# Gate projections of a decoder layer: each pass as two matmuls on the two row halves of TensorE's array

## The chip, the cores and the metric

The kernel runs on one core of one Trainium2 chip. The metric is the device time of one execution in microseconds (us). The profile's engines are PE (TensorE's matmuls), PEld (TensorE's loads of stationary weights), DVE (VectorE), ACT (ScalarE), POOL (GpSimd) and SP (the engine that issues most DMAs).

## The reference

One layer of a decoder trunk, with 512 tokens of 1024 channels, all in float32:

```python
h = rms_norm(x, g_pre_mix)
q, k, v, cb, cc, cu, ga, gc = split(h @ w_in)      # 512 x 6, then 1024 x 2 columns
y_attn = stick_breaking_attention(q, k, v) @ w_attn_out
y_conv = (cb * causal_depthwise_conv(cc * cu, w_conv)) @ w_conv_out
gate_attn, gate_conv = split(sigmoid(concat([ga, gc]) + b_gate))
x = x + rms_norm((gate_attn * y_attn + gate_conv * y_conv) @ w_o, g_post_mix)
x = x + rms_norm(square(relu(rms_norm(x, g_pre_mlp) @ w_up)) @ w_down, g_post_mlp)
x = x + sigmoid(rms_norm(x, g_ple) @ w_ple_gate) * (p @ w_ple_proj)
```

The change is in `ga` and `gc`: `h` (512 x 1024) times columns 3072 to 5119 of `w_in`.

## The kernel before, in words

Float32 precision is reached with three passes of a reduced format (float32r). Each operand is split into a high part, rounded to float32r by ScalarE, and a low part, the rest, made by VectorE (`split`, L63 to L65). A product is then high x high, high x low and low x high, added up in PSUM: `mm3`, whose three matmuls are lines L89, L90 and L91 wherever they are issued from.

`h` is held transposed, with channels on the 128 partitions and the 512 tokens along the free dimension, as eight blocks of 128 channels; `hx(k)` gives the high and low part of block k (`h1h` and `h1l` in the profile). `wcols` loads 128 columns of a weight matrix, eight blocks of 128x128, with one DMA into `raw` and splits them into `whi` and `wlo`. `proj` takes a bank of PSUM and runs the 8 x 3 = 24 matmuls of one projection onto it: the stationary operand is a 128x128 block of weights, the moving one 128x512 of `h`, and the contraction is over all 128 rows of the array.

`gate(j, which)` (L398 to L402) is one such projection for output channels 128j to 128j+127 of `ga` (which = 0) or `gc` (which = 1), and a sigmoid with its bias that ScalarE reads straight from the bank into an SBUF tile `tmp` (L401). There are 16 gates. The two of j = 0 are placed in the last round of the attention loop (L421 and L426). The others are in the mixing loop, `for j in range(NK)` at L448, which runs in this order: the gates of j, an output projection of the convolution branch (12 matmuls, `py`, L458) whose bank is multiplied into the gate by L459, an output projection of the attention branch (12 matmuls, L462) with L463, the addition of both (L464) and the split into `mh` and `ml` (L465). For j = 1 the first gate comes earlier, between the two output projections of j = 0 (L461), and the second at its own place; for j = 2 to 7 both gates stand side by side.

The order of TensorE's and SP's instructions is as written (`manual_schedule`); that of the other engines is drawn up by the framework's scheduler from its own costs. PSUM has eight banks, all given out in turn by `bank()`; `tm()` gives out one of five SBUF tiles of 128x512. In the mixing loop GpSimd also forms differences of `w_down` blocks (`make_sums`, L296), which are written to DRAM for a later stage. After the loop come eight transposes of the per-layer input (L477, their banks emptied by the split into `pt`) and the rows of W_o (`rows`, L481), whose first round takes all eight banks.

Of the kernel before, what the change touches and what calls it, by code (L numbers as in the profile page):

```python
# [12 lines left out]
ALU = mybir.AluOpType  # L13
# [3 lines left out]
P = 128  # L17
# [3 lines left out]
NK = D // P  # L21
# [12 lines left out]
def hybrid_block(ctx, tc, x, p, g_pre_mix, w_in, b_gate, w_conv, w_attn_out, w_conv_out, w_o,  # L34
                 g_post_mix, g_pre_mlp, w_up, w_down, g_post_mlp, g_ple, w_ple_gate, w_ple_proj, out):
    nc = tc.nc
# [4 lines left out]
    w_in, w_conv, w_attn_out, w_conv_out = w_in[0], w_conv[0], w_attn_out[0], w_conv_out[0]  # L41
# [15 lines left out]
    def bank():  # L57
        return psp.tile([P, 512], F32, tag="ps", name="ps")

    def tm(dt=F32):  # L60
        return tmp.tile([P, 512], dt, tag="tmp", name="tmp")
# [5 lines left out]
    def weights(loads, shape):  # L67
        raw = raws.tile(shape, F32, tag="raw", name="raw")
        for sel, src in loads(raw):
            nc.sync.dma_start(sel, src)  # L70
        lo = wts.tile(shape, F32R, tag="w", name="wlo")
        hi = wts.tile(shape, F32R, tag="w", name="whi")
        half = shape[1] // 2
        for sl in (slice(0, half), slice(half, 2 * half)):
            split(hi[:, sl], lo[:, sl], raw[:, sl])
        return hi, lo
# [4 lines left out]
    def wcols(w, c0):  # L81
        src = w[:, c0:c0 + P].rearrange("(k p) m -> p k m", p=P)
        return weights(lambda t: [(t, src)], [P, NK, P])
# [4 lines left out]
    def mm3(ps, lh, ll, rh, rl, start, stop, onto=False):  # L88
        nc.tensor.matmul(ps, lh, rh, start=start, stop=False, skip_group_check=onto)  # L89
        nc.tensor.matmul(ps, lh, rl, start=False, stop=False, skip_group_check=onto)  # L90
        nc.tensor.matmul(ps, ll, rh, start=False, stop=stop, skip_group_check=onto)  # L91

    def proj(w, xs, nk=NK, k0=0):
        ps = bank()
        for k in range(nk):
            xh, xl = xs(k)
            mm3(ps, w[0][:, k0 + k], w[1][:, k0 + k], xh, xl, k == 0, k == nk - 1)
        return ps
# [41 lines left out]
    def mov(hp):  # L140
        return lambda k: (hp[0][k // 4][:, k % 4, :], hp[1][k // 4][:, k % 4, :])
# [116 lines left out]
    for t in range(2, NT):  # L258
        ps = bank()
# [9 lines left out]
    hx = mov(h1)  # L269
# [126 lines left out]
        split(oy_h[1][:, c], oy_l[1][:, c], y)  # L396

    def gate(j, which):  # L398
        ps = proj(wcols(w_in, 3072 + 1024 * which + j * P), hx)
        sg = tm()  # L400
        nc.scalar.activation(sg, ps, AF.Sigmoid, bias=cols[:, 8 * which + j:8 * which + j + 1])  # L401
        return sg  # L402
# [9 lines left out]
    for j in range(4):  # L412
        wa = scores(st[0])
        wb = scores(st[1])
        y = conv_u(j, ct)
        conv_b(j, y)
        ta = wtrans(wa)
        if j < 3:
            st = proj_q(j + 1)
        else:  # L420
            sg[0] = gate(0, 0)  # L421
        tb = wtrans(wb)
        if j < 3:
            proj_k(j + 1, st)
        else:
            sg[1] = gate(0, 1)  # L426
        of = tm()
        with tc.high_priority(-LATE):
            make_sums(nc.vector)
        av(2 * j, ta, of)  # L430
        av(2 * j + 1, tb, of)
        if j < 3:
            ct = conv_c(j + 1)
# [14 lines left out]
    for j in range(NK):  # L448
        make_sums()
        sa, sc = sg if j == 0 else (next_gate if j == 1 else gate(j, 0), gate(j, 1))  # L450

        def two(t, j=j):
# [20 lines left out]
        if j == 7:  # L473
            for kk in range(2):
                ps = bank()
# [88 lines left out]
    for t in range(NT):  # L564
        tok = slice(t * P, (t + 1) * P)
        for h_ in range(2):
            cs = slice(h_ * 512, (h_ + 1) * 512)
            ps = bank()
# [21 lines left out]
    for half in range(2):  # L590
        ns = slice(half * 256, (half + 1) * 256)
        for c in (0, NJ):
# [3 lines left out]
            for k in range(NK):  # L596
                xh, xl = hm(k)
# [256 lines left out]
    for t in range(2, NT):  # L854
        for cs in CUTS[t]:
            ps = bank()[:, 0:cs.stop - cs.start]
# [31 lines left out]
```

## Time and profile before

| what | value |
|---|---|
| median of 2 runs | 746.5 us (746.45 to 746.55) |
| profiled execution, device time | 746.06 us |
| its span, first to last instruction | 744.0 us |
| mean granted TensorE clock | 0.993 |
| matmuls / weight loads | 3936 / 3936 |
| TensorE matmul busy | 730.5 us |
| VectorE busy | 539.1 us |
| ScalarE busy | 396.2 us |

The device time is 2.1 us longer than the span, since it holds what lies around the first and the last instruction. In the profile's rows, busy time is the sum of shown durations; matmuls are pipelined, so one matmul's shown duration is longer than the distance to the next one's start, and the distance between starts (the pitch) is what counts for time. Rows of the order in time give the start and the duration in us, the engine, the line, the operation, the tiles (written <- read), rows*columns of the array, shape and count; what stands in brackets is the engine's idle time before it and what ended that.

### The profile page before, as it was taken

Reading aid. Unit: us, or ns where it says so; the run is one execution under the profiler, and the core shown is the slowest. Engines: PE = TensorE matmul, PEld = TensorE weight load, DVE = VectorE, ACT = ScalarE, POOL = GpSimd, SP = SyncE. Lnnn points to the kernel's source line nnn. Section 1 sums busy time; section 2 is a strip of 40 time slices with the busy share of each in tenths; the row PEclk is TensorE's granted clock in tenths of the full one; section 3 lists DMA queues with packets and bytes.
Section 4 is the critical chain, followed back from the end, with each engine's and each line's share of the span. In section 5 each row is a group of like instructions: output and inputs, shape, how many; then the busy total and the mean of one; then the engine's idle time right before and its main releaser. Section 6 shows DMA issues by size and latency. Waiting matters only on the chain.

```text
span 744.0 us, 10442 instructions
## 1 busy us (share of the span) xinstructions
PE 730.5 (98%) x3936; PEld 632.4 (85%) x3936; DVE 539.1 (72%) x747; ACT 396.2 (53%) x672; POOL 108.0 (15%) x131
## 2 busy tenths in 40 slices
PE   7999999998999999999999999999999999999997
PEld 6888788887888888878899999999988888888876
DVE  4889898959755424554869879977699878268762
ACT  6555656462533322442855776867776476256531
POOL 0005051347425222200100000000000000001100
PEclk8999999999999999999999999999999999999999
DMA  8393727157599885752244444432555767577311
GB/s 310 126 327 107 221 100 227 54 199 252 178 346 273 254 281 193 269 161 57 106 178 112 115 115 114 118 110 86 168 160 174 224 243 230 174 245 263 128 58 58
DMA packets 112107, 132.30 MB, mean 178 GB/s; under 512 B 4116, under 2 KB 82744, under 8 KB 111032
## 3 DMA queue, kind: packets, MB, share of 16 engines
q1 hardware_dynamic: 111480, 127.44, 53.8%
q10 hardware_dynamic: 576, 4.19, 1.4%
q8 instruction: 31, 0.51, 0.3%
q14 instruction: 20, 0.16, 0.1%
HBM read 108.55 MB, written 23.07 MB: 177 GB/s over the span
## 4 chain that ended last, share of the span: by engine, by line
PE 82%; DVE 6%; DMA 5%; ACT 3%; POOL 2%; issue 1%; SPq 1%; DVEq 0%; POOLq 0%; ACTq 0%
PE ps L89 26%; PE ps L90 26%; PE ps L91 26%; DVE wlo L65 1%; DMA w<-in_w_down_dram 1%; DMA raw<-wsum 1%; PE ps L368 1%; POOL w L296 1%; DMA xin<-in_x_dram 1%; DMA wsum<-w 1%; DMA raw<-in_w_o_dram 1%; ACT whi L64 1%; DVE keep L338 1%; PE ps L354 1%; PE ps L548 1%
## 5 line engine op out<-in xcount | busy, mean ns | idle before, releaser
L65 DVE TENSOR_TENSOR wlo<-raw,whi 128x512 fp32r<-128x512 f32 x120 | 89.4, 776 | 45.8 <-ACT whi L64 19.7
L89 PE MATMUL ps<-h1h,whi 128*128 128x512 f32 x288 | 113.8, 395 | 2.7 <-DVE tmp L395 2.7
L91 PE MATMUL ps<-h1h,wlo 128*128 128x512 f32 x288 | 112.8, 392 | 0.0
L90 PE MATMUL ps<-h1l,whi 128*128 128x512 f32 x288 | 112.7, 391 | 0.0
L64 ACT CAST whi<-raw 128x512 fp32r<-128x512 f32 x120 | 69.1, 638 | 49.6 <-DMA raw<-in_w_in_dram 16.0
L89 PE MATMUL ps<-w,sb 128*128 128x512 f32 x216 | 84.1, 389 | 0.0
L91 PE MATMUL ps<-w,sb 128*128 128x512 f32 x216 | 84.0, 389 | 0.0
L90 PE MATMUL ps<-w,sb 128*128 128x512 f32 x216 | 84.0, 389 | 0.0
L65 DVE TENSOR_TENSOR w<-raw,w 128x1024 fp32r<-128x1024 f32 x56 | 67.7, 1222 | 22.0 <-PE ps L90 11.6
L64 ACT CAST w<-raw 128x1024 fp32r<-128x1024 f32 x56 | 58.4, 1051 | 37.5 <-DMA raw<-wsum 13.4
L125 POOL TENSOR_TENSOR rs<-ms,mhalf 128x1 f32<-128x1 f32 x20 | 14.5, 726 | 409.0 <-DVE ms L121 367.6
L89 PEld LDWEIGHTS ps<-h1h,whi 128*128 128x128 f32 x288 | 54.5, 189 | 13.8 <-DVE tmp L395 2.9
L91 PEld LDWEIGHTS ps<-h1h,wlo 128*128 128x128 f32 x288 | 54.3, 189 | 11.5
L90 PEld LDWEIGHTS ps<-h1l,whi 128*128 128x128 f32 x288 | 54.6, 189 | 11.0
L89 PE MATMUL ps<-h2h,us 128*128 128x256 f32 x224 | 63.5, 283 | 0.0
L90 PE MATMUL ps<-h2l,us 128*128 128x256 f32 x224 | 63.4, 283 | 0.0
L91 PE MATMUL ps<-h2h,us 128*128 128x256 f32 x224 | 63.4, 283 | 0.0
L65 DVE TENSOR_TENSOR us<-raw,us 128x1024 fp32r<-128x1024 f32 x42 | 50.7, 1219 | 7.9 <-ACT us L64 7.7
L64 ACT CAST us<-raw 128x1024 fp32r<-128x1024 f32 x42 | 43.4, 1050 | 19.1 <-DVE raw L647 7.5
L89 PE MATMUL ps<-tb,us 128*128 128x256 f32 x168 | 47.9, 285 | 0.0
L90 PEld LDWEIGHTS ps<-w,sb 128*128 128x128 f32 x216 | 40.5, 188 | 8.5
L89 PEld LDWEIGHTS ps<-w,sb 128*128 128x128 f32 x216 | 40.5, 188 | 8.4
(206 smaller groups left out, 1715.6 us busy)
## 6 DMA issues: line engine op xcount, KB each, us to landing
raw<-in_w_in_dram SPq DMA_DIRECT2D x36, 512.0 KB, 6.9
w<-in_w_down_dram SPq DMA_DIRECT2D x32, 512.0 KB, 4.3
wsum<-w SPq DMA_DIRECT2D x32, 512.0 KB, 3.8
raw<-in_w_up_dram SPq DMA_DIRECT2D x32, 512.0 KB, 4.5
raw<-wsum SPq DMA_DIRECT2D x32, 512.0 KB, 5.1
raw<-in_w_down_dram SPq DMA_DIRECT2D x24, 512.0 KB, 4.3
raw<-in_w_o_dram SPq DMA_DIRECT2D x8, 512.0 KB, 6.0
raw<-in_w_ple_gate_dram SPq DMA_DIRECT2D x8, 512.0 KB, 6.7
```

The lines of the kernel that those rows point to most:

```text
L64: nc.scalar.copy(hi, src)
L65: nc.vector.tensor_tensor(lo, src, hi.bitcast(F32), op=ALU.subtract)
L89: nc.tensor.matmul(ps, lh, rh, start=start, stop=False, skip_group_check=onto)
L90: nc.tensor.matmul(ps, lh, rl, start=False, stop=False, skip_group_check=onto)
L91: nc.tensor.matmul(ps, ll, rh, start=False, stop=stop, skip_group_check=onto)
L125: nc.gpsimd.tensor_tensor(r, m, mhalf, op=ALU.pow)
L296: eng.tensor_tensor(r, x_, y_, op=ALU.subtract)
L338: nc.vector.tensor_tensor_scan(kr, kr, kr, 1.0, op0=ALU.mult, op1=ALU.bypass)
L354: nc.tensor.transpose(ps[:, c0 + (qb - kb) * P:c0 + (qb - kb + 1) * P], w[:, o:o + P], ident)
L368: nc.tensor.matmul(ps[:, kb * P:S], lhs, wt[i][:, c0:c0 + n], start=(kb == 0 and i == 0), stop=(kb == NT - 1 and i == 1))
L548: nc.tensor.transpose(ps[:, i * P:(i + 1) * P], hn1[t][g][:, i * P:(i + 1) * P], ident)
```

## The change

For all gates but the two of j = 0, the eight blocks' three passes are issued as two matmuls each: one over contraction rows 0 to 63, one over rows 64 to 127, with the same 128 output channels and 512 tokens. The first half of the rows adds up in one PSUM bank, the second in another. ScalarE then copies the first bank to an SBUF tile, VectorE adds the second bank to it, and the sigmoid reads that tile in place of the bank.

```diff
     def gate(j, which):
-        ps = proj(wcols(w_in, 3072 + 1024 * which + j * P), hx)
+        w = wcols(w_in, 3072 + 1024 * which + j * P)
+        if j == 0:
+            ps = proj(w, hx)
+        else:
+            part = [bank(), bank()]
+            for k in range(NK):
+                xh, xl = hx(k)
+                for i, (lhs, rhs) in enumerate(((w[0][:, k], xh), (w[0][:, k], xl), (w[1][:, k], xh))):
+                    for h in range(2):
+                        rows_ = slice(64 * h, 64 * h + 64)
+                        nc.tensor.matmul(part[h], lhs[rows_], rhs[rows_], start=(k == 0 and i == 0),
+                                         stop=(k == NK - 1 and i == 2))
+            ps = tm()
+            nc.scalar.copy(ps, part[0])
+            nc.vector.tensor_tensor(ps, part[1], ps, op=ALU.add)
         sg = tm()
         nc.scalar.activation(sg, ps, AF.Sigmoid, bias=cols[:, 8 * which + j:8 * which + j + 1])
         return sg
```

The loads, the DMAs and the split of the weights stay as they are; the order of the gates and projections does too.

## The prediction

> **What bounds the kernel now.** I read the page's busy table and its chain first, then the busy time of each engine by stage, then the order in time of single matmuls inside one gate.
>
> ```profile
> span 744.0 us, 10442 instructions
> ...
> PE 730.5 (98%) x3936; PEld 632.4 (85%) x3936; DVE 539.1 (72%) x747; ACT 396.2 (53%) x672; POOL 108.0 (15%) x131
> ...
> PE 82%; DVE 6%; DMA 5%; ACT 3%; POOL 2%; issue 1%; SPq 1%; DVEq 0%; POOLq 0%; ACTq 0%
> ```
>
> TensorE is busy for 98% of the span and carries 82% of the chain that ended last. A busy TensorE says little by itself, so the stage and the pitch (start to start) have to be seen. Of the 16 gates, the two with j = 0 run before 200 us and stay as they are; the other 14 lie between 200 and 312 us.
>
> ```profile
> core 0: us, PE busy (x) PEld busy (x) DVE busy (x) ACT busy (x) POOL busy (x), PEclk, DMA share, GB/s
> 186.00:200.00 14.00, 13.87 (x61) 11.18 (x60) 13.94 (x19) 9.82 (x19) 6.38 (x4) 0.93 0.72 231
> 200.00:312.00 112.00, 112.00 (x495) 92.74 (x495) 51.96 (x66) 35.04 (x58) 36.70 (x28) 1.00 0.79 256
> ```
>
> In this stage TensorE never pauses (112.00 of 112.00 us, full clock), while VectorE is busy for 51.96 us and ScalarE for 35.04 us of it. Whatever the change adds to TensorE here goes straight into the end of the kernel; what it adds to the other two has 60 and 77 us of idle time to lie in. Now one gate, that of j = 1, first and last matmul with the weight loads between them:
>
> ```profile
> 205.95 0.39 PE L89 MATMUL ps<-h1h,whi 128*128 128x512 f32 x1
> 205.96 0.19 PEld L90 LDWEIGHTS ps<-h1l,whi 128*128 128x128 f32 x1
> ...
> 206.18 0.39 PE L90 MATMUL ps<-h1l,whi 128*128 128x512 f32 x1
> 206.18 0.19 PEld L91 LDWEIGHTS ps<-h1h,wlo 128*128 128x128 f32 x1
> 206.41 0.39 PE L91 MATMUL ps<-h1h,wlo 128*128 128x512 f32 x1
> ...
> 211.17 0.39 PE L91 MATMUL ps<-h1h,wlo 128*128 128x512 f32 x1
> ...
> 211.39 0.39 PE L89 MATMUL ps<-oyh,whi 128*128 128x512 f32 x1
> ```
>
> The gate is 24 matmuls (8 blocks of contraction rows, three passes each) from 205.95 to 211.39: 5.44 us, a **pitch of 0.2267 us** a pass. The 0.39 us shown for one is its whole way through the array, of which 0.16 us lies under the next. Each load starts as the matmul before it starts, lies wholly beside it, and costs nothing. The 14 changed gates hold 14 x 24 = 336 passes, 76.2 us.
>
> **The change, part by part.** Each pass becomes two loads and two matmuls of 64 rows and the same 512 columns. No instruction with 64 contraction rows is in this trace, so whether the two run beside each other can't be read from it; all of the argument is in bounds. Per pass two costs must be held apart: the streaming of 512 columns, and the loads.
>
> Streaming, from the matmuls of 256 columns in the up projection, 12 of them from the first row to the last:
>
> ```profile
> 420.37 0.28 PE L89 MATMUL ps<-h2h,us 128*128 128x256 f32 x1
> ...
> 421.81 0.28 PE L89 MATMUL ps<-tb,us 128*128 128x256 f32 x1
> ```
>
> 1.44 / 12 = 0.120 us. So 256 columns more cost 0.1067 us, 512 columns 0.213 us, and 0.0133 us is fixed for each matmul. If the halves stream beside each other, a pass can't take less than 0.213 us (336 x 0.0133 = 4.5 us gained) and, if both fixed parts are paid one after the other, takes 0.240 us (4.5 us lost).
>
> Loads, from the place where they are the limit, the short matmuls of attention:
>
> ```profile
> 153.81 0.19 PEld L368 LDWEIGHTS ps<-wth,v 128*128 128x128 f32 x1
> 153.93 0.23 PE L368 MATMUL ps<-wth,v 128*128 128x128 f32 x1
> 153.93 0.19 PEld L368 LDWEIGHTS ps<-wtl,v 128*128 128x128 f32 x1
> 153.99 0.27 PE L368 MATMUL ps<-wtl,v 128*128 128x128 f32 x1
> 154.04 0.19 PEld L368 LDWEIGHTS ps<-wth,v 128*128 128x128 f32 x1
> 154.10 0.44 PE L368 MATMUL ps<-wth,v 128*128 128x512 f32 x1
> 154.16 0.19 PEld L368 LDWEIGHTS ps<-wtl,v 128*128 128x128 f32 x1
> ...
> 154.38 0.39 PE L368 MATMUL ps<-wtl,v 128*128 128x512 f32 x1
> ```
>
> Loads follow each other at 0.11 to 0.12 us, although each is shown as 0.19, and a matmul may start 0.06 us after its load started. Two loads in a pass, with 128 columns each as now, take 0.22 to 0.23 us at this rate if fewer rows make them no shorter: **just inside** the 0.2267 us. A workable order exists: the matmul of the upper half starts, the lower half's load runs for 0.11 us, its matmul starts, the upper half's next load runs for 0.11 us, and then the upper half's stream is just done. So for overlapping halves I take a pass at 0.2267 us, **0 us**, with -4.5 and +4.5 as ends. The row nearest to it, the 256-column one, keeps 0.120 us with a load each; two of these would be 0.240, the upper end, but there the streaming sets the pitch, which here is shared.
>
> Switches between whole-height and half-height work: j = 1 has its two gates apart, between output projections, j = 2 to 7 side by side, so 2 x 8 = 16 entries and exits. Least 0; at most the array empties (0.39 - 0.2267 = 0.16 us) and the next load follows unhidden (0.19 us), 0.35 us. Between these ends I take the emptying alone, with the load under it, as the loads lie in the gate's rows: 16 x 0.16 = **2.6 us** (0 to 5.6). The Trainium skill ("TensorEngine Tiling (Array Packing)", Key Properties) states that a change of the tiling mode drains TensorE; by it 2.6 us is the least of this term, where rows of a stream that never breaks would give 0 and a sum 2.6 us lower. No row here shows such a switch.
>
> Taking the sum out of the banks: each gate adds a ScalarE copy and a VectorE addition of 128x512 and makes the sigmoid wait for both.
>
> ```profile
> L380 ACT COPY tmp<-ps x4: 586/587/590, 55.6 to 162.4; 128x512 f32<-128x512 f32 x4
> ...
> L463 DVE TENSOR_TENSOR tmp<-tmp,ps x8: 680/686/689, 206.2 to 317.6; 128x512 f32<-128x512 f32 x8
> ...
> L401 ACT ACTIVATE tmp<-ps,cols x16: 679/689/695, 188.2 to 309.5; 128x512 f32<-128x512 f32 x16
> ```
>
> 14 x 0.587 = 8.2 us on ScalarE and 14 x 0.686 = 9.6 us on VectorE, in idle time of 77 and 60 us. The sigmoid comes about 1.3 us later than now; its user, the product L459, needs the output projection of 12 passes (2.7 us) behind the second gate anyway. While ScalarE waits with copy and sigmoid, the casts of the next weights (L64) are queued behind them, and their users are matmuls a gate or more later. TensorE waits in this stretch for nothing now, and the banks, six a round in place of four, come round only after eight: the first gate's two are written again by the next round's second gate, 72 passes or 16 us after they are full, and need some 2 us to be read. The one place without cover is the first rows of W_o:
>
> ```profile
> PE ps L89 <- DVE tmp L395: 2.7, 1, 2.7
> ...
> PE ps L89 <- DVE pt L65: 0.2, 1, 0.2
> ```
>
> ```profile
> 312.30 0.69 DVE L459 TENSOR_TENSOR tmp<-tmp,ps 128x512 f32<-128x512 f32 x1 [0.45 <-PE ps L91]
> 315.07 2.58 DVE L65 TENSOR_TENSOR wlo<-raw,whi 128x512 fp32r<-128x512 f32 x4 [2.08 <-ACT whi L64]
> ```
>
> TensorE waits there 0.2 us for a bank that VectorE empties. Both additions of j = 7 (1.4 us) fall ahead of the 2.08 us in which VectorE idles for the weights of W_o, so they cost **0**; if they land behind it, 1.4 us. Less than nothing is possible too, since ScalarE's and VectorE's order is drawn up anew: the 2.7 us wait at about 190 us, and the 7% of clock lost in 186 to 200 us (1.0 us), could go; in the other direction such a wait could arise anew.
>
> Sum: 0 + 2.6 + 0 = 2.6 us on the profiled execution's 746.06 us, 748.7; the median of the runs, 746.5, is 0.4 above that execution, so **749 us**. Its own range: 746.5 - 4.5 = 742 below, 746.5 + 4.5 + 5.6 + 1.4 = 758 above.
>
> **The rivals.**
>
> Serial halves, **slower**. If the second half's matmul starts only when the first has streamed, because the array takes one matmul at a time or the operands' rows don't give each half a place of its own (the change then doesn't do what it says), each pass is two of 0.2267 us: 336 x 0.2267 = 76.2 us, 822.7, with the switches 825. For it: in the rows above no matmul starts before the columns of the one ahead have streamed; the 128-column ones, 0.06 us apart, are merely short. Against it: every matmul there takes all the rows, so that none had a free place to start in; with half the rows free, the order worked out above needs nothing but that TensorE uses them. The Trainium skill ("TensorE: Matmul & The Clock Gate", Part 3, The mechanism) has matmuls on different row groups start about 4 ns apart and overlap; by it a pass costs nothing more, and no run so far shows it.
>
> Exposed loads, **slower**. If in half-height work a load may not lie beside a matmul of its own half, each half's turn is a stream and a load, 0.2267 + 0.11 us, also when the halves overlap: 336 x 0.11 = 37.0 us, with the switches 786 us. Against it stands that at 205.96 the load starts 0.01 us after a matmul on the same rows and costs nothing. The same section of the Trainium skill says that loads overlap with matmuls in flight only when the row group differs, which is this rival's rule; this trace contradicts it for whole-height work and shows nothing for halves.
>
> From 0.271 us a pass (15 us over 336 passes) the result leaves the 2%. Something between is a fourth case: if loads come late, as for the matmul shown at 154.10, whose next starts 0.28 us after it, a pass costs 0.053 us more, 18 us in all, 765 us and up. A gain over 2% would need 15 us; streaming alone gives 4.5 us at most, and the lost waits 3.7 us.
>
> **How the numbers follow.** Overlap at 749 us: 0.60. Serial, 825 us: 0.20. Exposed loads, 786 us: 0.14. Something between: 0.04. Over 2% faster: 0.02. The range reaches from the forecast's low end past the exposed loads with the forecast's upper bounds in part, 742 to 790, and leaves out the serial case and the gain. Two per cent, 15 us, is about what a measurement of this kernel can tell from no change; within it lies only the overlap, 0.60, and slower are the three others, 0.38.
>
> **What would show it.** Overlap: in a changed gate, matmuls of 64 rows start 48 to a gate within 5.4 to 5.8 us, the two of a pass side by side or some 0.11 us apart, and the stage from 200 us on keeps its 112 us but for a few. Serial: matmuls 0.227 us apart all along, a gate of 10.9 us. Exposed loads: gates of about 8.1 us, each load starting after the stream of its own half. Switches: a gap over 0.227 us at the first and last matmul of a gate. The additions are wrong as costed if TensorE waits in the stage for L459, for the copies or for a bank. The forecast falls with one row: halves of one pass that never overlap.

## The result, and the profile after

The changed kernel takes 750.4 us (median of 750.0 and 750.9) against 746.5 us: ratio 1.0061, 95% interval 1.0036 to 1.0085. That is no change by the 2% of the forecast, and 4 us of loss that the interval can tell from nothing. The forecast was 749 us, its range 742 to 790 us.

First the page after: the span, the busy table, the chain.

```profile
span 749.1 us, 11169 instructions
...
PE 734.4 (98%) x4272; PEld 630.6 (84%) x4272; DVE 551.2 (74%) x761; ACT 405.5 (54%) x686; POOL 109.2 (15%) x131
...
PE 80%; DVE 6%; DMA 6%; POOL 2%; ACT 2%; issue 2%; SPq 1%; POOLq 0%; DVEq 0%; ACTq 0%
```

There are 336 matmuls more (4272 for 3936), and TensorE's busy time rises by 3.9 us only. The gate of j = 1 in order of time, in the view that holds TensorE's matmuls and loads; x2 joins two instructions that start together, and 64*128 is rows*columns of the array:

```profile
206.24 0.39 PE L91 MATMUL ps<-oyh,wlo 128*128 128x512 f32 x1
206.55 0.18 PEld L409 LDWEIGHTS ps<-h1h,whi 64*128 64x128 f32 x2 [0.35 <-PE ps L90]
206.56 0.50 PE L409 MATMUL ps<-h1h,whi 64*128 64x512 f32 x2
206.66 0.19 PEld L409 LDWEIGHTS ps<-h1l,whi 64*128 64x128 f32 x2
...
206.89 0.40 PE L409 MATMUL ps<-h1l,whi 64*128 64x512 f32 x2
...
211.70 0.39 PE L409 MATMUL ps<-h1l,whi 64*128 64x512 f32 x2
...
211.92 0.39 PE L409 MATMUL ps<-h1h,wlo 64*128 64x512 f32 x2
212.24 0.19 PEld L89 LDWEIGHTS ps<-oyh,whi 128*128 128x128 f32 x1 [0.35 <-PE ps L409]
212.24 0.50 PE L89 MATMUL ps<-oyh,whi 128*128 128x512 f32 x1
212.35 0.19 PEld L90 LDWEIGHTS ps<-oyl,whi 128*128 128x128 f32 x1
...
212.58 0.40 PE L90 MATMUL ps<-oyl,whi 128*128 128x512 f32 x1
```

The two matmuls of a pass start together, and so do their two loads: **the halves overlap in full**. At the gate's end a pass is 0.22 to 0.23 us, as before. The gate takes 206.56 to 212.24 = 5.68 us in place of 5.44, and the 0.24 us sit at its edges. At an entry or exit the next matmul starts 0.32 us after the last one in place of 0.227, and its load starts only with it (before, it started a matmul earlier), so that this load isn't hidden: the matmul's row is 0.50 us long in place of 0.39, and the matmul behind it comes 0.33 to 0.34 us later, 0.11 us more than in the stream.

To see where the 4 us are, I set every pass of TensorE against the same pass of before (the two halves of a pass as one). The difference of their start times is 0.02 us at the last pass ahead of the first changed gate and 3.96 us behind the last: **16 switches at 0.247 us, 3.95 us**, and nothing between them. It then grows to 5.90 us in the first round of W_o, 1.94 us more, and falls to 5.20 us by the end. W_o's start, in TensorE's waits and in the order of ScalarE and VectorE:

```profile
PE ps L89 <- DVE pt L65: 0.8, 1, 0.8
...
PE ps L89 <- DVE tmp L473: 0.5, 1, 0.5
...
PE ps L89 <- DVE tmp L477: 0.2, 1, 0.2
```

```profile
310.29 1.91 ACT L64 CAST wph<-wpr 128x2048 fp32r<-128x2048 f32 x1
317.15 1.14 ACT L64 CAST whi<-raw 128x512 fp32r<-128x512 f32 x2 [4.95 <-DMA raw<-in_w_o_dram]
318.52 1.14 ACT L64 CAST whi<-raw 128x512 fp32r<-128x512 f32 x2 [0.24 <-DMA raw<-in_w_o_dram]
319.57 0.58 ACT L412 COPY tmp<-ps 128x512 f32<-128x512 f32 x1
```

```profile
317.80 2.67 DVE L65 TENSOR_TENSOR wlo<-raw,whi 128x512 fp32r<-128x512 f32 x4 [2.92 <-ACT whi L64]
320.39 0.68 DVE L413 TENSOR_TENSOR tmp<-ps,tmp 128x512 f32<-128x512 f32 x1
322.26 0.69 DVE L473 TENSOR_TENSOR tmp<-tmp,ps 128x512 f32<-128x512 f32 x1 [1.19 <-ACT tmp L415]
```

The last gate's first whole-height successor starts at 313.1 us, so both its banks are full by then; yet ScalarE copies the first at 319.57 (L412), because the casts of W_o's rows are queued ahead of it and the engine idles 4.95 us for their DMA. The addition (L413), the sigmoid and the two products (L473, L477) that free banks come late in a row, and TensorE waits for the banks of W_o's first round.

### The profile page after: what moved, and what is told of

Its sections match the earlier page's. It is cut to its first block, busy times and chain, and to the rows that moved or that the text cites. A ratio compares the mean times of both kernels' runs of the same rounds, so it can differ in the third digit from the quotient of the medians.

```text
span 749.1 us, 11169 instructions
## 1 busy us (share of the span) xinstructions
PE 734.4 (98%) x4272; PEld 630.6 (84%) x4272; DVE 551.2 (74%) x761; ACT 405.5 (54%) x686; POOL 109.2 (15%) x131
## 4 chain that ended last, share of the span: by engine, by line
PE 80%; DVE 6%; DMA 6%; POOL 2%; ACT 2%; issue 2%; SPq 1%; POOLq 0%; DVEq 0%; ACTq 0%
PE ps L89 23%; PE ps L90 23%; PE ps L91 23%; PE ps L409 9%; POOL w L296 1%; DMA raw<-in_w_o_dram 1%; DVE wlo L65 1%; DMA w<-in_w_down_dram 1%; DMA xin<-in_x_dram 1%; DMA raw<-in_w_conv_out_dram 1%; DMA wsum<-w 1%; DMA raw<-in_w_up_dram 1%; DVE keep L338 1%; ACT whi L64 1%; PE ps L354 1%
## 5 line engine op out<-in xcount | busy, mean ns | idle before, releaser
L65 DVE TENSOR_TENSOR wlo<-raw,whi 128x512 fp32r<-128x512 f32 x120 | 90.4, 784 | 31.0 <-ACT whi L64 14.7
L90 PE MATMUL ps<-w,sb 128*128 128x512 f32 x216 | 84.0, 389 | 0.0
L65 DVE TENSOR_TENSOR w<-raw,w 128x1024 fp32r<-128x1024 f32 x56 | 67.6, 1222 | 21.5 <-PE ps L90 14.2
L89 PE MATMUL ps<-h1h,whi 128*128 128x512 f32 x176 | 70.2, 399 | 3.0 <-DVE tmp L395 3.0
L91 PE MATMUL ps<-h1h,wlo 128*128 128x512 f32 x176 | 69.2, 393 | 0.0
L90 PE MATMUL ps<-h1l,whi 128*128 128x512 f32 x176 | 69.1, 393 | 0.0
L90 PE MATMUL ps<-h2l,us 128*128 128x256 f32 x224 | 63.4, 283 | 0.0
L65 DVE TENSOR_TENSOR us<-raw,us 128x1024 fp32r<-128x1024 f32 x42 | 50.7, 1220 | 7.5 <-ACT us L64 7.5
L89 PE MATMUL ps<-tb,us 128*128 128x256 f32 x168 | 47.7, 284 | 0.4 <-ACT tmp L680 0.4
L89 PEld LDWEIGHTS ps<-w,sb 128*128 128x128 f32 x216 | 40.5, 188 | 8.5
L90 PEld LDWEIGHTS ps<-w,sb 128*128 128x128 f32 x216 | 40.5, 188 | 8.4
L91 PEld LDWEIGHTS ps<-w,sb 128*128 128x128 f32 x216 | 40.5, 188 | 8.4
L91 PE MATMUL ps<-tb,us 128*128 128x256 f32 x168 | 47.5, 283 | 0.0
L90 PE MATMUL ps<-tb,us 128*128 128x256 f32 x168 | 47.5, 283 | 0.0
```

The costliest lines, as they stand in the source:

```text
L65: nc.vector.tensor_tensor(lo, src, hi.bitcast(F32), op=ALU.subtract)
```

## The experiments

The times of before in these runs lie between 739 and 749 us from one execution to the next. One trace of before is kept; the traces of the runs below differ from one another by up to 3.8 us at the first changed gate, and nearly all of that has arisen in the first 20 us. So the ratios are to be compared, and the differences within one stage. A stage's cost is worked out as above, from the start times of the passes against those of before. The expected times were reckoned from a before of 746.5 us.

**The changed kernel again.**

> The changed kernel once more, as the measure for the runs beside it. Theory (the halves overlap in full; paid are 16 switches between whole-height and half-height work, and a late emptying of one gate's banks ahead of W_o): 16 x 0.2465 = 3.9 us, 2.1 us at W_o, some 1 us given back later, 750 to 751 us. Rival (each half-height pass is a little dearer, 0.012 us x 336): the same 750 to 751 us; this run doesn't tell them apart.

Measured: 749.7 us against 743.7, ratio 1.0088 (1.0057 to 1.0120). The stage with the gates again costs 3.95 us, W_o's start 1.4 us.

**More switches.**

```diff
-    for h in range(2): ...two matmuls of 64 rows
+    if k % 2 == 0:
+        nc.tensor.matmul(part[0], lhs, rhs, ...)      # all 128 rows
+    else:
+        for h in range(2): ...two matmuls of 64 rows
```

> Blocks of contraction rows alternate between whole-height (even) and half-height (odd), so 8 switches a gate, 112 in place of 16, and half as many half-height passes (168). Theory: 96 more switches at 0.20 to 0.25 us (some of the 0.2465 us is spread over the passes behind a switch, which here come only three at a time): +19 to +24 us on the changed kernel, 769 to 775 us. Rival, a price of each half-height pass: half of the 3.9 us goes, 748 to 749 us. By the prediction's 0.16 us a switch: +15 us, 766 us.

Measured: 769.1 us, ratio 1.0347 (1.0315 to 1.0378), 19.4 us over the changed kernel beside it. From the first gate to the last the stage costs 24.1 us for 112 switches, 0.215 us each. Rows of it in order of time:

```profile
198.91 0.39 PE L408 MATMUL ps<-h1h,wlo 128*128 128x512 f32 x1
199.23 0.19 PEld L412 LDWEIGHTS ps<-h1h,whi 64*128 64x128 f32 x2 [0.36 <-issue]
199.23 0.50 PE L412 MATMUL ps<-h1h,whi 64*128 64x512 f32 x2
199.34 0.19 PEld L412 LDWEIGHTS ps<-h1l,whi 64*128 64x128 f32 x2
199.57 0.39 PE L412 MATMUL ps<-h1l,whi 64*128 64x512 f32 x2
```

Half the half-height passes and seven times the switches cost six times as much. The price belongs to the switch: the next matmul starts 0.09 us late, the one behind it a further 0.11 us (the load that isn't hidden), and some 0.05 us are spread over the passes after that when there are enough of them. The rival, a price of each pass, is out.

**Both on the same half.**

```diff
-    rows_ = slice(64 * h, 64 * h + 64)
+    rows_ = slice(0, 64)
```

> Both matmuls of a pass take rows 0 to 63 (rows 64 to 127 are left out of the gates and rows 0 to 63 counted twice), with all else as in the change. Theory (two matmuls overlap because they stand on different rows): they now follow each other, each load beside the matmul ahead: 336 x 0.2267 = 76 us on the changed kernel, 826 us. With exposed loads, by the prediction's rival: each matmul 0.2267 + 0.11 us, 150 us more, 900 us. Rival (the array takes two matmuls at once wherever they stand): 750 us.

Measured: 823.7 us, ratio 1.1077 (1.1026 to 1.1128). By the ratios (1.1077 less 1.0088) that is 74 us over the changed kernel; from the first gate to the last the stage costs 79.9 us, 75.9 more than in the changed kernel, where the theory had 76. In the rows x2 now joins two that follow each other:

```profile
198.16 0.63 PE L409 MATMUL ps<-h1l,whi 64*128 64x512 f32 x2
198.40 0.42 PEld L409 LDWEIGHTS ps<-h1h,wlo 64*128 64x128 f32 x2
198.63 0.38 PE L409 MATMUL ps<-h1h,wlo 64*128 64x512 f32 x1
```

A matmul of 64 rows costs as much as one of 128, and two run at once only when they stand on different rows of the array. The loads stay hidden all the same: but for those at the gates' edges, each one starts 0.002 to 0.004 us after a matmul on its own half and lies beside it, so the rival of exposed loads is out for half-height work too.

**Three and three.**

```diff
-    for i, (lhs, rhs) in enumerate(...):
-        for h in range(2):
+    for h in range(2):
+        for i, (lhs, rhs) in enumerate(...):
```

> The same 48 matmuls a gate, but the three of the upper half of a block, then the three of the lower half. Theory (matmuls start in the order in which they are written, and overlap only with a neighbour on the other half): of six matmuls, the last of one half lies beside the first of the other, four turns of 0.2267 us for three passes: 112 x 0.2267 = 25.4 us more, 776 us. Rival (TensorE looks ahead and starts a later matmul whose half is free): no change, 750 to 751 us. Rival (overlap only within a pair that shares the pass): 76 us more, 826 us.

Measured: 750.7 us, ratio 1.0101 (1.0073 to 1.0130), as the changed kernel. My theory's order of starts was **wrong**, and so was the rival that ties overlap to the pair:

```profile
195.08 0.50 PE L409 MATMUL ps<-h1h,whi 64*128 64x512 f32 x2
...
195.42 0.40 PE L409 MATMUL ps<-h1l,whi 64*128 64x512 f32 x2
...
195.65 0.40 PE L409 MATMUL ps<-h1h,wlo 64*128 64x512 f32 x2
```

Written as upper 1, 2, 3, lower 1, 2, 3, they start as upper 1 with lower 1, 2 with 2, 3 with 3, the lower one 0.010 us later: TensorE started the fourth matmul ahead of the second and third.

**How far ahead.**

```diff
-    for k in range(NK): ...for i...: for h in range(2):
+    for h, k in [(h, k) for h in range(2) for k in range(NK)]: ...for i...:
```

> The same 48 matmuls a gate, first all 24 of the upper half, then all 24 of the lower. The runs in threes showed that a matmul starts ahead of earlier ones that wait for their half; this asks how far that goes. Theory A (each half has a queue of its own and TensorE looks at least 24 matmuls and their loads ahead): no change, 749 to 751 us. Theory B (it looks only a few ahead, n matmuls): in each gate the first lower one starts when 24 - n upper ones have, so that (24 - n) x 0.2267 us a gate are added, 14 gates, less where a pair's second gate starts its upper half beside the first one's lower: for n = 8 up to 51 us more, for n = 3 up to 67 us. The number of upper ones that start ahead of the first lower one is read from the rows.

> As the run before, but in two blocks: twelve upper, twelve lower, twelve upper, twelve lower. Theory A: no change, 749 to 751 us. Theory B, for n under 12: (12 - n) turns of 0.2267 us at a gate's start and again at its end or middle, up to 14 x 2 x 4 x 0.2267 = 25 us more for n = 8, and nothing for n of 12 and over, so that with the run before it brackets n.

Measured: 811.7 us, ratio 1.0897 (1.0871 to 1.0923), and for the twelves 786.0 us, ratio 1.0556 (1.0521 to 1.0591). In the first gate of the run with all upper ones ahead, matmuls start one by one from 196.92 us on; these rows are the 20th, the 21st and what follows:

```profile
201.38 0.39 PE L409 MATMUL ps<-h1l,whi 64*128 64x512 f32 x1
...
201.61 0.39 PE L409 MATMUL ps<-h1h,wlo 64*128 64x512 f32 x1
201.61 0.19 PEld L409 LDWEIGHTS ps<-h1h,whi 64*128 64x128 f32 x2
201.62 0.61 PE L409 MATMUL ps<-h1h,whi 64*128 64x512 f32 x2
```

The first lower matmul starts 0.007 us after the 21st of 24 upper ones, that is with three upper ones still waiting. Among the twelves it starts 0.006 us after the ninth of 12, with three waiting again. So n = 3, theory B: a matmul may pass three that wait for the other half and no more. Whether the count is one of matmuls or of their loads these rows don't tell, since the lower load too starts only at 201.61.

The cost agrees. From the first gate to the last the two stages cost 65.1 and 43.3 us, so 61.1 and 39.4 without the 3.95 us of the switches, where all halves one after the other would cost 76.2. The first run has 20 places at which one half's stretch ends beside the start of the other's (14 within gates, 6 between gates side by side), the second 48; each saves 0.76 and 0.77 us, a little over three turns of 0.2267. (My formula was one turn a gate too high: the first lower matmul runs beside the 21st upper one, so 20 and not 21 run alone.)

**The emptying without the halves.**

```diff
-    for h in range(2): ...two matmuls of 64 rows
+    nc.tensor.matmul(part[k % 2], lhs, rhs, ...)      # all 128 rows
```

> Whole-height matmuls as before, but even blocks add up in one bank and odd ones in another, with the same copy and addition as in the change: the emptying without the halves. Theory: no switches, 3.9 us less than the changed kernel; the wait ahead of W_o stays if the order of ScalarE and VectorE is the same: 746.5 to 748.5 us. Rival, the copy and the addition cost most of the 4 us (through waits at many places): 749 to 750.5 us.

Measured: 743.6 us, ratio 0.9996 (0.9980 to 1.0013). By the ratio that is 746.2 us where before takes 746.5, just under the theory's range; the rival's 749 us lies outside the interval. The stage with the gates costs 0.00 us more than before: the 14 copies and additions are hidden there. W_o's start does cost 1.4 us of the profiled execution, 1.2 of which are back by its end. It comes about in another way than in the changed kernel, though:

```profile
316.24 2.00 DVE L65 TENSOR_TENSOR wlo<-raw,whi 128x512 fp32r<-128x512 f32 x3 [1.95 <-ACT whi L64]
318.15 0.68 DVE L475 TENSOR_TENSOR tmp<-tmp,ps 128x512 f32<-128x512 f32 x1
```

The last gate's copy (309.10 us) and addition (312.13) run ahead of W_o's casts here; what stands behind W_o's splits on VectorE is the last product (L475). ScalarE's first cast behind its wait for W_o's rows starts 0.86 us after W_o's first matmul, where in before it starts 1.14 us ahead of it. Why these weights come later isn't settled.

**The halves without the emptying.**

```diff
-    ps = tm(); nc.scalar.copy(ps, part[0]); nc.vector.tensor_tensor(ps, part[1], ps, op=ALU.add)
+    ps = part[0]
```

> The halves as in the change, but the copy and the addition are left out: the sigmoid reads the first bank, so the lower half of the contraction is left out of the gates' result. Theory: the 16 switches stay (3.9 us), the 2.1 us at W_o go: 749 to 750.5 us, with the order's small gains and losses of 1 us either way. Rival (the copy and the addition cost most of the change): 746.5 to 747.5 us.

Measured: 747.8 us against 744.4, ratio 1.0057 (1.0032 to 1.0083), 4.2 us by the ratio and 3.4 by the medians; the rival's 0 to 1 us is out. The stage costs 3.95 us, W_o's start 0.07 us, though the last sigmoid stands behind W_o's casts here too (316.32 us). With the run before it: the loss of the stage is the switches alone; the emptying's part is a wait at one place.

**The last copy ahead of W_o's casts.**

```diff
-    wk = wrow(w, k)
+    with tc.issue_after(last_copy), tc.issue_after(last_addition):      # k >= 2
+        wk = wrow(w, k)
```

> The changed kernel with the casts of W_o's rows 2 to 7 queued behind the last gate's copy on ScalarE and behind its addition on VectorE. Theory (the copy and the addition come late because those casts wait for their DMA ahead of them): TensorE's three waits at the start of W_o, 2.1 us in all beyond those of before, go: 1.5 to 2.2 us less than the changed kernel, 748 to 749 us. Rival (TensorE waits there because VectorE and ScalarE have too much to do): no gain, or the weights of W_o come late in their turn: 750 us or more.

Measured: 748.3 us against 743.7, ratio 1.0064 (1.0043 to 1.0086). With a before of 743.7 and not 746.5 it is the gain that counts: 1.4 us below the changed kernel beside it, where the theory had 1.5 to 2.2; the two intervals overlap, so the time alone doesn't settle it. The trace does: over W_o's start the difference to before falls by 0.53 us (the wait for `pt` that before has there is gone too), in place of a rise of 1.4 to 1.9 us. ScalarE's order there:

```profile
309.68 1.91 ACT L64 CAST wph<-wpr 128x2048 fp32r<-128x2048 f32 x1 [0.37 <-PE ps L411]
312.67 0.59 ACT L414 COPY tmp<-ps 128x512 f32<-128x512 f32 x1 [1.08 <-PE ps L411]
313.15 1.14 ACT L64 CAST whi<-raw 128x512 fp32r<-128x512 f32 x2
```

The copy starts 0.2 us after the first matmul behind the last gate (312.51 us), in place of 6.5 us, and TensorE's waits on L473, L477 and `pt` are gone. In the changed kernel it was the queue's order, not the load of the two engines.

**Quarters.**

```diff
-    part = [bank(), bank()]
+    n = 4 if which == 0 else 2      # rows P // n * h to P // n * (h + 1), n - 1 additions
+    part = [bank() for _ in range(n)]
```

> In the first gate of each j over 0 each pass is four matmuls of 32 rows into four banks (with three additions), in the second two of 64 as in the change. Theory (loads on different rows run beside each other, as the pairs' starts 0.003 to 0.004 us apart show): a pass stays at 0.2267 us; at most six more switches, between quarters and halves, of 0.25 us, and 14 more additions: 750 to 754 us. Rival (loads share one path at 0.11 us each, and two just fitted): four loads a pass are 0.44 us, 168 x 0.21 = 36 us more, 786 us.

Measured: 751.7 us against 744.4, ratio 1.0124 (1.0083 to 1.0165). That is 7.3 us by the medians and 9.2 by the ratio, where the theory's range has 3.5 to 7.5 and the rival 39.5: the rival is out, and the theory is right for the stage but short at W_o's start.

```profile
194.56 0.40 PE L410 MATMUL ps<-h1l,whi 32*128 32x512 f32 x4
194.57 0.20 PEld L410 LDWEIGHTS ps<-h1h,wlo 32*128 32x128 f32 x4
194.80 0.40 PE L410 MATMUL ps<-h1h,wlo 32*128 32x512 f32 x4
194.80 0.19 PEld L410 LDWEIGHTS ps<-h1h,whi 32*128 32x128 f32 x4
```

Four matmuls, and four loads, start within 0.010 to 0.020 us of each other in all 168 passes, so loads on different rows don't share a path of 0.11 us each. The stage costs 5.24 us: 16 switches and six more between quarters and halves, at 0.24 us each. W_o's start costs 4.4 us: the last gate's copy (318.32 us) and its one addition (320.90) stand behind W_o's casts and splits again, and some 1 us of it lies in matmuls that start 0.43 us apart, where the granted clock fell (0.72 over 320 to 326 us).

## Why the prediction was right

*What bounds the kernel.* Right: what TensorE lost in the gates' stage and at W_o's start came out at the end, less 0.7 us.

*Streaming.* 0 us, as taken, between -4.5 and +4.5: no pass changed its pitch. The upper end, both fixed parts of 0.0133 us paid in a row, doesn't occur, nor does the gain.

*Loads.* Right in the sum and **wrong in the working**. I let the two loads of a pass follow each other, 0.22 us in a turn of 0.2267, and built an order for it with the halves 0.11 us apart. They run beside each other; the quarters show that there was room for four.

*Switches.* **This term was mis-sized**: 2.6 us at 0.16 each, measured 3.95 us at 0.247, inside its 0 to 5.6 us. I took the emptying alone with the load under it. In the runs the next matmul doesn't start 0.16 us late but 0.09, and its load is exposed (0.11 us), which I had only in the upper bound; the 0.05 us spread behind it I didn't have at all. The rule of the Trainium skill ("TensorEngine Tiling (Array Packing)", Key Properties) that a change of mode drains TensorE agrees in direction: the trace has the 0.09 us of wait at every one of the 16 edges.

"No row here shows such a switch" was wrong: the trace of before holds a matmul of 28 rows (L266) amid whole-height ones.

```profile
38.49 0.39 PE L91 MATMUL ps<-vh,h1l 128*128 128x512 f32 x1
38.81 0.13 PEld L266 LDWEIGHTS ps<-ident,crow 28*128 28x128 f32 x1 [0.35 <-PE ps L90]
38.81 0.24 PE L266 MATMUL ps<-ident,crow 28*128 28x28 f32 x1
...
38.98 0.19 PEld L89 LDWEIGHTS ps<-h1h,whi 128*128 128x128 f32 x1
38.98 0.50 PE L89 MATMUL ps<-h1h,whi 128*128 128x512 f32 x1
...
39.32 0.39 PE L90 MATMUL ps<-h1l,whi 128*128 128x512 f32 x1
```

It has the marks of the gates' edges: a start 0.32 us after the one ahead with the load only then, and on the way back a row of 0.50 us with the next start 0.34 us later. Read beforehand, these rows would have given some 0.2 us a switch (0.09 and 0.11) and 3.2 us for the term.

*Emptying the banks.* 0 us taken, 1.4 us as the other end; in the profiled execution 1.94 us, in the second one of the changed kernel 1.4, at the place named as the one without cover and by the mechanism named for the other end (behind the idle time for W_o's weights). The choice of 0 failed because I placed both additions ahead of that idle time and counted them alone: the last copy stands in ScalarE's queue behind the same weights, and the addition, the sigmoid and two products follow it in a chain. Elsewhere the term held: the stage cost nothing.

*Given back.* 0.7 us of the difference is gone by the end; before, TensorE waited 0.6 us for the low part of the last stage's weights (L90 for DVE L65), and after, the list of its waits has no such row. That some of a loss is absorbed by later waits wasn't in the sum. It isn't steady either: the second profile of the changed kernel gets as much back there (0.78 us) but loses 0.8 and 0.4 us at two waits between 400 and 510 us, so that 5.5 us are left at its end. In the first one the terms add up to 5.9 us, 5.2 are left at the last instruction, and the time is 4.8 us longer, as 0.3 less lies outside the span than before. So it is in part **luck** that 750.4 came so near to 749: two terms were too small by 1.4 and 1.9 us, and 1.1 us that nobody forecast came off.

*The rivals.* Serial halves: what it would have cost is measured by the run on one half, 824 us (825 forecast); with different rows it doesn't happen. Something between: no pass but those behind an edge takes more than its 0.2267 us, so it doesn't occur. The Trainium skill ("TensorE: Matmul & The Clock Gate", Part 3, The mechanism) gives starts about 4 ns apart; the trace has 0.003 to 0.004 us. Exposed loads: contradicted with both halves and with one; that section's rule, loads beside matmuls only when the row group differs, doesn't hold here. The Trainium skill also has matmuls start strictly in order there; the three runs on the order of the halves contradict it.

## What to carry to other kernels

Splitting a contraction over the array's rows took no more of TensorE's time here, at 512 columns, and gains nothing where all rows were in use; what it costs is the number of changes between row heights, 0.2 to 0.25 us each, so matmuls of one height belong side by side. An added copy or sum is hidden in a stage only if it also stands ahead, in its engine's queue, of the work that waits for a DMA: look at the last one of the stage, not the mean. Two streams on different rows may be written up to three matmuls apart and still overlap; written further apart they ran one after the other, but for the last few.

## What the runs showed of the hardware that I had not expected

Matmuls pass each other: one whose rows are free starts ahead of up to three earlier ones that wait, 0.006 to 0.010 us after the one that runs. Loads for different rows run beside each other, four at once within 0.020 us, though loads for all rows follow each other at 0.11 us. And a change between quarters and halves costs as much as one between halves and the whole, 0.24 us.
